# Rotary embedding over split heads: GpSimd's sine products taken two rows at a time

## The chip, the cores and the metric

The kernel runs on one core of a Trainium2 chip. The metric is the device time of the whole kernel in microseconds (us); lower is better. Three runs of the kernel before gave 161.14, 161.40 and 161.66 us, median 161.4 us.

## The reference

`x` is 16 batches x 512 positions x 1024 numbers (16 heads of 64), `cos` and `sin` are 512 x 32, everything fp32. Each head is split into halves x1 and x2 of 32 numbers, and

```
x    = x.reshape(16, 512, 16, 64);  x1, x2 = x[..., :32], x[..., 32:]
cos  = cos[None, :, None, :];       sin = sin[None, :, None, :]
out  = concatenate([x1*cos - x2*sin,  x1*sin + x2*cos], axis=-1)
```

So each number costs two products and a sum: its own value by the cosine, and its partner in the other half by plus or minus the sine. 33.6 MB are read and 33.6 MB are written.

## The kernel before, in words

**Rows.** The work is cut into 64 rows, numbered u = 0 to 63 (lists `rows`, `NU`). A row is 128 partitions x 1024 numbers: 4 KB in each partition. A tile is a load and a store: the first two and the last two batches are single tiles of 4 rows (2 MB), the twelve between go in six pairs of 8 rows (4 MB). Rows 0-3 and 4-7 are tiles 0 and 1, rows 8-15 to 48-55 are tiles 2 to 7, rows 56-59 and 60-63 are tiles 8 and 9. `x_sb` is a ring of 40 rows; results are written over the inputs and stored from there. Tiles 0 to 5 fill the ring and are loaded at once; tiles 6 to 9 wait for earlier stores.

**What a row goes through.**
- `mul` (VectorE, line 293): x times cosine into one of three PSUM buffers (`t1_ps`, NT1 = 3, slot u mod 3). It waits until row u-3 has left that buffer.
- The sine product: x with its halves swapped (a reversed axis, `::-1`) times the signed sine table, into one of six SBUF buffers (`t2_sb`, NT2 = 6, slot u mod 6). GpSimd does it at line 257 for 58 rows; VectorE does it at line 286 for the six rows that `V2` marks (r = 3 of each 8-row tile: 11, 19, 27, 35, 43, 51).
- The sum, in one of two ways. For 43 rows VectorE adds both products into `x_sb` (`comb`, line 304). For the 21 rows that `PE2` marks (4 <= u < 60 and u mod 8 in 1, 3, 6) TensorE adds the sine product into the PSUM buffer with a multiplication by the identity (line 224: two calls, four instructions), and ScalarE copies the buffer to `x_sb` (line 191).

**Order on the engines.** Each engine runs its list in order. VectorE's is written at line 311: for each u, `mul(u)` and then `comb(u-1)` unless row u-1 is TensorE's. Over eight rows of a tile, by r: mul0, comb7 of the tile before, mul1, comb0, mul2, (sine product 3) mul3, comb2, mul4, mul5, comb4, mul6, comb5, mul7. Because `t1_ps` has three slots, mul of r = 1 waits for ScalarE's copy of r = 6 of the tile before, mul4 for that of r = 1, mul6 for that of r = 3.

GpSimd goes through its 58 rows in order. Before each product it waits for the row's tile to be loaded (at r = 0, semaphore `sem_in`) and until row u-6 has released the slot of `t2_sb` (`wait_t2_free`, line 139): TensorE's semaphore `sem_e` if u-6 was a TensorE row, else VectorE's `sem_v` of that row's `comb`. After each product it counts up `sem_p`; `n_pool[u]` is the count that row u's reader waits for.

Loads are issued on ScalarE's queue (line 153), the later ones between its copies: after the copy of row 17, 25 and 33, with a wait for an earlier store (lines 192 to 195). Stores are issued on SyncE's queue (line 161) when a tile's last row and all before it are summed.

Of the kernel before, what the change touches and what calls it, by code (L numbers as in the profile page):

```python
# [6 lines left out]
def bass_split_heads_rope_kernel(  # L7
# [17 lines left out]
    H = int(num_heads)  # L25
    HD = dim // H
    HALF = HD // 2
    P = 128
    R1 = seq // P
# [5 lines left out]
    mult = mybir.AluOpType.mult  # L35
# [5 lines left out]
    tiles = [(b, R1 if b in singles else R2) for b in range(batch) if b in singles or b % 2 == 0]  # L41
# [4 lines left out]
    NU = len(rows)  # L46
# [5 lines left out]
    V2 = [tiles[t][1] == R2 and r == V_ROW for t, r in rows]  # L52

    def count(flags):
        return [sum(flags[: u + 1]) for u in range(NU)]

    n_pool = count([not v for v in V2])
    n_pe = count(PE2)
    n_comb = count([not a for a in PE2])

    NT1 = 3
    NT2 = 6
# [5 lines left out]
    with ExitStack() as stack:  # L68
        x_sb = stack.enter_context(nc.sbuf_tensor([P, RING, H, 2, HALF], fp32))
        t2_sb = stack.enter_context(nc.sbuf_tensor([P, NT2, H, 2, HALF], fp32))  # L70
        stage = stack.enter_context(nc.sbuf_tensor([P, 2, R1 * HALF], fp32))
        s1_sb = stack.enter_context(nc.sbuf_tensor([P, R1, 2, HALF], fp32))
        s2_sb = stack.enter_context(nc.sbuf_tensor([P, R2, 2, HALF], fp32))
# [17 lines left out]
        sem_m = stack.enter_context(nc.semaphore("mul"))  # L91
# [8 lines left out]

        def c_of(t, r):
            return c1_ps[:, r, :] if tiles[t][1] == R1 else pair_ps[:, r // R1, 0, r % R1, :]

        def s_of(t, r):
            return s1_sb[:, r] if tiles[t][1] == R1 else s2_sb[:, r]

        x1 = x.rearrange("b (s r) d -> b s (r d)", r=R1)
        o1 = out.rearrange("b (s r) h d -> b s (r h d)", r=R1)
# [13 lines left out]
        def where(u):  # L122
            t, r = rows[u]
            return t, r, u % RING

        def swapped(k):
            return x_sb[:, k, :, ::-1, :]

        def over_heads(table):
            return table[:, None, :, :].broadcast_to([P, H, 2, HALF])  # L130
# [8 lines left out]
        def wait_t2_free(eng, u):  # L139

            if u >= NT2:
                v = u - NT2
                if PE2[v]:
                    eng.wait_ge(sem_e, n_pe[v])
                else:
                    eng.wait_ge(sem_v, n_comb[v])
# [87 lines left out]
        def on_gpsimd(pl):  # L234
            pl.memset(ident[:], 1.0).then_inc(sem_i, 1)  # L235
            pl.wait_ge(sem_i, 1)
            pl.affine_select(  # L237
                out=ident[:],
                in_=ident[:],
                compare_op=mybir.AluOpType.is_equal,  # L240
                fill=0.0,
                base=0,
                pattern=[[-1, P]],
                channel_multiplier=1,
            ).then_inc(sem_i, 1)
            for u in range(NU):
                if V2[u]:
                    continue
                t, r, k = where(u)
                if (t, r) == (0, 0):  # L250
                    pl.wait_ge(sem_s, 1)
                if (t, r) == (2, 0):
                    pl.wait_ge(sem_s, 2)
                if r == 0:
                    pl.wait_ge(sem_in[t], 16)
                wait_t2_free(pl, u)
                pl.tensor_tensor(  # L257
                    t2_sb[:, u % NT2, :, :, :], swapped(k), over_heads(s_of(t, r)), mult
                ).then_inc(sem_p, 1)

        def on_vector(ve):
# [55 lines left out]
        on_sync(nc.sync)  # L317
        on_scalar(nc.scalar)
        on_gpsimd(nc.gpsimd)
        on_tensor(nc.tensor)  # L320
        on_vector(nc.vector)
# [33 lines left out]
```

## Time and profile before

| | |
|---|---|
| runs, us | 161.14, 161.40, 161.66 (median 161.4) |
| profiled execution: first to last instruction (span) | 160.3 us; its time with what lies around the span is not given apart, and the three runs lie 0.8 to 1.3 us above it |
| GpSimd, sine products, line 257 | x58, 2346 ns each, 134.2 us |
| VectorE, cosine products, line 293 | x64, 1.22 us each |
| VectorE, sums, line 304 | x43, 1.22 us each |
| VectorE, sine products, line 286 | x6, 1.21 us each |
| TensorE, sine into PSUM, line 224 | x84 instructions for 21 rows |
| ScalarE, copies, line 191 | x21, 1.02 us each |
| bytes moved | 67.26 MB, mean 419 GB/s over the span |
| loads / stores | 6 of 4 MB and 4 of 2 MB / the same |

The profile is of one execution. "Busy" counts the instructions of an engine; the number behind "idle before" is the time in which the engine stood still ahead of an instruction, and the name behind the arrow is what ended it. A timeline line reads: start, duration (of the whole merged group), engine, line, operation, written<-read, shapes, count.

### The profile page before, as it was taken

The numbers are of one execution on the slowest core, as the hardware profiler recorded it, in microseconds if no ns is written. First come the engines' busy times: TensorE is split into PE (matmuls) and PEld (weight loads), VectorE is DVE, ScalarE is ACT, GpSimd is POOL, SyncE is SP. The second block draws the span as 40 slices with busy tenths as digits, with TensorE's granted clock in tenths as the row PEclk, the third lists the DMA queues.
The fourth block names the chain that finished last, engine by engine and source line by source line (L and its number), as shares of the span: only waits on it lengthen the run. The fifth ranks groups of instructions, "written<-read, shape, count | busy, mean of one in ns | idle before, by whom it ended". The sixth has DMA issues, their size and how long they took to land.

```text
span 160.3 us, 522 instructions
## 1 busy us (share of the span) xinstructions
PE 72.8 (45%) x94; PEld 24.0 (15%) x94; DVE 130.3 (81%) x117; ACT 24.4 (15%) x27; POOL 134.9 (84%) x64
## 2 busy tenths in 40 slices
PE   6050004478357936660847105489458435850000
PEld 1020002022202211210221002022202111220000
DVE  0069998599989999996999709899889999999500
ACT  0420000203120222022012010201220402040000
POOL 1059999999999999999999999699999999289400
PEclk9955555557755587689687965555555977699555
DMA  5999999999999999999999999999999999999896
GB/s 147 409 441 474 409 450 409 425 429 429 446 429 458 417 411 466 409 433 401 450 433 425 425 409 458 409 433 433 411 429 462 441 417 401 450 441 441 376 450 294
DMA packets 3170, 67.26 MB, mean 419 GB/s; under 512 B 352, under 2 KB 608, under 8 KB 608
## 3 DMA queue, kind: packets, MB, share of 16 engines
q10 hardware_dynamic: 1728, 33.69, 49.6%
q1 hardware_dynamic: 1440, 33.56, 48.9%
q14 instruction: 2, 0.02, 0.0%
HBM read 33.69 MB, written 33.55 MB: 419 GB/s over the span
## 4 chain that ended last, share of the span: by engine, by line
DMA 60%; POOL 13%; DVE 8%; PE 7%; issue 3%; ACT 2%; ACTq 1%; DVEq 0%
DMA x_sb<-in_x_dram 41%; DMA out_dram<-x_sb 18%; POOL t_sb L257 13%; PE t_ps L224 7%; DVE t_ps L293 5%; DVE x_sb L304 3%; ACT x_sb L191 2%; ACTq L153 1%; ACTq L174 1%; DVE t_sb L286 0%; DVEq L303 0%
## 5 line engine op out<-in xcount | busy, mean ns | idle before, releaser
L257 POOL TENSOR_TENSOR t_sb<-x_sb,s_sb 128x1024 f32<-128x1024 f32 x58 | 134.2, 2346 | 14.8 <-ACT s_sb L183 8.5
L224 PE MATMUL t_ps<-t_sb,ident 128*128 128x512 f32 x84 | 68.0, 957 | 63.0 <-DVE t_ps L293 39.2
L293 DVE TENSOR_TENSOR t_ps<-x_sb,pair_ps 128x1024 f32<-128x1024 f32 x48 | 57.7, 1223 | 9.9 <-ACT x_sb L191 9.8
L304 DVE TENSOR_TENSOR x_sb<-t_ps,t_sb 128x1024 f32<-128x1024 f32 x43 | 52.4, 1218 | 2.6 <-POOL t_sb L257 2.6
L224 PEld LDWEIGHTS t_ps<-t_sb,ident 128*128 128x128 f32 x84 | 22.1, 290 | 108.9 <-DVE t_ps L293 74.6
L191 ACT ACTIVATE x_sb<-t_ps 128x1024 f32<-128x1024 f32 x21 | 21.5, 1023 | 109.9 <-PE t_ps L224 96.9
L293 DVE TENSOR_TENSOR t_ps<-x_sb,tab_ps 128x1024 f32<-128x1024 f32 x16 | 19.3, 1222 | 0.1
L286 DVE TENSOR_TENSOR t_sb<-x_sb,tab_ps 128x1024 f32<-128x1024 f32 x6 | 7.3, 1213 | 0.0
L264 DVE COPY tab_ps<-stage 128x128 f32<-128x128 f32 x1 | 0.3, 294 | 7.8 <-DMA stage<-in_cos_dram 7.8
L208 PE MATMUL pair_ps<-stage,pick 128*128 128x256 f32 x4 | 2.0, 667 | 5.4 <-DMA stage<-in_sin_dram 5.4
L201 PE MATMUL t_ps<-zero 128*128 128x512 bf16 x6 | 2.7, 627 | 1.3 <-DVE zero L262 1.3
L208 PEld LDWEIGHTS pair_ps<-stage,pick 128*128 128x128 f32 x4 | 1.2, 324 | 6.4 <-issue 6.3
L177 ACT ACT_TABLE_LOAD x1 | 1.3, 1283 | 5.5 <-issue 5.5
L201 PEld LDWEIGHTS t_ps<-zero 128*128 128x128 bf16 x6 | 0.7, 136 | 2.4 <-DVE zero L262 1.2
L262 DVE MEMSET zero<- 128x256 uint32 x1 | 0.3, 272 | 0.9 <-PEq L337 0.9
L186 ACT ACTIVATE s_sb<-pair_ps 128x256 f32<-128x256 f32 x1 | 0.4, 383 | 1.7 <-PE pair_ps L208 1.7
L182 ACT ACTIVATE s_sb<-stage 128x128 f32<-128x128 f32 x1 | 0.3, 309 | 2.1 <-DMA stage<-in_sin_dram 2.1
L235 POOL MEMSET ident<- 128x128 f32 x1 | 0.2, 204 | 0.3 <-POOLq L337 0.3
L177 ACT ACTIVATE pick<-ident 128x256 f32<-128x256 f32 x1 | 0.4, 416 | 0.0
L187 ACT ACTIVATE s_sb<-pair_ps 128x256 f32<-128x256 f32 x1 | 0.4, 379 | 0.0
L237 POOL TENSOR_SCALAR_AFFINE_SELECT ident<-ident 128x128 f32<-128x128 f32 x1 | 0.3, 292 | 0.1
L337 POOL MEMSET const-float32-0.0<- 128x1 f32 x1 | 0.1, 98 | 0.3 <-issue 0.3
(6 smaller groups left out, 1.0 us busy)
## 6 DMA issues: line engine op xcount, KB each, us to landing
x_sb<-in_x_dram ACTq DMA_DIRECT2D x6, 4096.0 KB, 38.0
out_dram<-x_sb SPq DMA_DIRECT2D x6, 4096.0 KB, 25.0
x_sb<-in_x_dram ACTq DMA_DIRECT2D x4, 2048.0 KB, 22.6
out_dram<-x_sb SPq DMA_DIRECT2D x4, 2048.0 KB, 15.2
stage<-in_cos_dram ACTq DMA_DIRECT2D x1, 64.0 KB, 7.8
stage<-in_sin_dram ACTq DMA_DIRECT2D x1, 64.0 KB, 7.5
```

What stands on the lines that cost most here:

```text
L153: eng.dma_start(in_sbuf(t), in_dram(x1, x2, t)).then_inc(sem_in[t], 16)
L174: ae.dma_start(stage[:, i, :], table.rearrange("(s r) d -> s (r d)", r=R1)).then_inc(sem, 16)
L177: ae.activation(pick[:], ident[:].rearrange("q (s k) -> q k s", k=2)[:, :, :, None].broadcast_to([P, 2, P // 2, 2]), COPY).then_inc(sem_g, 1)
L186: ae.activation(s2[:, :, :, 0, :], pair_ps[:, :, 1, :, :], COPY, scale=-1.0)
L191: ae.activation(xs[:, u % RING, :], t1_ps[:, u % NT1, :], COPY).then_inc(sem_a, 1)
L201: pe.matmul(t1_ps[:, k, b * BANK:(b + 1) * BANK], zero[:, 0:P], zero[:], start=True, stop=True).then_inc(sem_w, 1)
L208: pe.matmul(pair_ps[:, k].rearrange("p c r d -> p (c r d)"), pick[:, k].rearrange("q s b -> q (s b)"), stage[:].rearrange("q c f -> q (c f)"),
L224: ins = pe.matmul(t1_ps[:, u % NT1, b * BANK:(b + 1) * BANK], ident[:], t2[:, b * BANK:(b + 1) * BANK], start=False, stop=True, skip_group ...
L257: pl.tensor_tensor(t2_sb[:, u % NT2, :, :, :], swapped(k), over_heads(s_of(t, r)), mult).then_inc(sem_p, 1)
L286: ve.tensor_tensor(t2_sb[:, u % NT2, :, :, :], swapped(k), over_heads(v_ps), mult)
L293: ve.tensor_tensor(t1_ps[:, u % NT1, :].rearrange("p (h d) -> p h d", d=HALF), x_sb[:, k, :, :, :].rearrange("p h t d -> p (h t) d"), c_of ...
L304: ve.tensor_tensor(xs[:, k, :], t1_ps[:, u % NT1, :], t2_sb[:, u % NT2, :, :, :].rearrange("p h t d -> p (h t d)"), add,).then_inc(sem_v, 1)
```

## The change

For a row u that is even, from 4 to 60, and not followed by a row of VectorE's (`joined`), GpSimd writes the sine products of u and u+1 with one instruction of 128 x 2048 elements into two neighbouring slots of `t2_sb`. There are 23 such pairs; 12 rows stay single (0 to 3, r = 2 of each 8-row tile, 62, 63), so 58 instructions become 35. In an 8-row tile the pairs are r = 0+1, 4+5, 6+7.

The wait for the slots changes with it. A pair with u+1 >= 6 no longer waits for the exact release of its slots; it waits once, for `sem_m` >= u - 1, which is the end of `mul(u-2)` on VectorE. (That mul itself had to wait until row u-5 had left its PSUM buffer, and so until row u-5's reader was through with `t2_sb`.) Single rows wait as before. Readers of u and of u+1 both wait for the one count that the pair's instruction makes.

```diff
-    n_pool = count([not v for v in V2])
+    def joined(u):
+        return u % 2 == 0 and R1 <= u < NU - 2 and not V2[u + 1]
+
+    G2 = [joined(u) or (u % 2 == 1 and joined(u - 1)) for u in range(NU)]
+    n_pool = count([not v and not (g and u % 2 == 1) for u, (v, g) in enumerate(zip(V2, G2))])
...
-                if V2[u]:
+                if V2[u] or (G2[u] and u % 2 == 1):
                     continue
                 t, r, k = where(u)
+                n = 2 if G2[u] else 1
...
-                wait_t2_free(pl, u)
+                if n == 2 and u + 1 >= NT2:
+                    pl.wait_ge(sem_m, u + 2 - NT2 + NT1)
+                elif n == 1:
+                    wait_t2_free(pl, u)
+                table = (s1_sb if tiles[t][1] == R1 else s2_sb)[:, r:r + n]
                 pl.tensor_tensor(
-                    t2_sb[:, u % NT2, :, :, :], swapped(k), over_heads(s_of(t, r)), mult
+                    t2_sb[:, u % NT2:u % NT2 + n],
+                    x_sb[:, k:k + n, :, ::-1, :],
+                    table[:, :, None, :, :].broadcast_to([P, n, H, 2, HALF]),
+                    mult,
                 ).then_inc(sem_p, 1)
```

More of the change, by code (lines that the diff above doesn't have):

```diff
@@ L102, in c_of @@
             return c1_ps[:, r, :] if tiles[t][1] == R1 else pair_ps[:, r // R1, 0, r % R1, :]
-        def s_of(t, r):
-            return s1_sb[:, r] if tiles[t][1] == R1 else s2_sb[:, r]
         x1 = x.rearrange("b (s r) d -> b s (r d)", r=R1)
```

## The prediction

> **What bounds the kernel now.** I read the page's busy shares and slices, then VectorE's and GpSimd's timelines, then the waits of the store queue.
>
> ```profile
> PE 72.8 (45%) x94; PEld 24.0 (15%) x94; DVE 130.3 (81%) x117; ACT 24.4 (15%) x27; POOL 134.9 (84%) x64
> ...
> POOL 1059999999999999999999999699999999289400
> ...
> DMA  5999999999999999999999999999999999999896
> ```
>
> The DMA engines are full from the second slice to the third last, so bytes (67.26 MB) set the floor. GpSimd has no gap until 100 us, and then a few. To lose time, the change has to delay the last store until the store queue runs dry; to gain, it has little room: the DMA's last slices (8, 9, 6) leave about 1 us.
>
> How much cover has the last store? In the trace it is issued at 151.70. The store of rows 56-59, ahead of it in the queue, lands at 155.48, the last at 160.31; its first packet starts at 154.28. So it waited in line, and a delay of one to three us may cost nothing.
>
> Now the compute that leads to that issue. VectorE's timeline in a late tile (rows 43 to 49):
>
> ```profile
> 109.53 2.35 DVE L293 TENSOR_TENSOR t_ps<-x_sb,pair_ps 128x1024 f32<-128x1024 f32 x2
> 111.79 1.22 DVE L304 TENSOR_TENSOR x_sb<-t_ps,t_sb 128x1024 f32<-128x1024 f32 x1
> 113.42 1.23 DVE L293 TENSOR_TENSOR t_ps<-x_sb,pair_ps 128x1024 f32<-128x1024 f32 x1 [0.41 <-ACT x_sb L191]
> 114.56 1.22 DVE L304 TENSOR_TENSOR x_sb<-t_ps,t_sb 128x1024 f32<-128x1024 f32 x1
> 115.69 2.35 DVE L293 TENSOR_TENSOR t_ps<-x_sb,pair_ps 128x1024 f32<-128x1024 f32 x2
> 117.95 1.22 DVE L304 TENSOR_TENSOR x_sb<-t_ps,t_sb 128x1024 f32<-128x1024 f32 x1
> 119.58 1.23 DVE L293 TENSOR_TENSOR t_ps<-x_sb,pair_ps 128x1024 f32<-128x1024 f32 x1 [0.41 <-ACT x_sb L191]
> ```
>
> These are mul44+45, comb44, mul46, comb45, mul47+48, comb47, mul49. VectorE starts an operation every 1.13 us (113.42, 114.56, 115.69), so its 14 operations per 8-row tile take 15.9 us. Twice here it stands 0.41 us for ScalarE's copy: mul46 ends at 114.65, TensorE starts row 46 at 114.70, ScalarE copies it from 118.52 to 119.54, and mul49 starts at 119.58. That way (4.93 us from mul end to the next mul) is already 0.41 us longer than what VectorE has to do meanwhile. **Any delay of TensorE's row r = 6 goes straight into VectorE.** GpSimd's timeline at the same place:
>
> ```profile
> 101.72 9.29 POOL L257 TENSOR_TENSOR t_sb<-x_sb,s_sb 128x1024 f32<-128x1024 f32 x4 [1.78 <-PE t_ps L224]
> 111.39 6.97 POOL L257 TENSOR_TENSOR t_sb<-x_sb,s_sb 128x1024 f32<-128x1024 f32 x3 [0.38 <-DMA x_sb<-in_x_dram]
> 118.56 18.54 POOL L257 TENSOR_TENSOR t_sb<-x_sb,s_sb 128x1024 f32<-128x1024 f32 x8 [0.21 <-PE t_ps L224]
> 141.02 9.27 POOL L257 TENSOR_TENSOR t_sb<-x_sb,s_sb 128x1024 f32<-128x1024 f32 x4 [3.92 <-DMA x_sb<-in_x_dram]
> ```
>
> Rows 44 to 47 are done from 101.72 to 111.01, row 46 by 108.70: some 6 us before TensorE takes it up. At the end GpSimd has finished row 59 and waits 3.92 us for the last load.
>
> **Cost of a pair.** Four rows took 9.27 us: a start every 2.31 us, 2.346 us each. Two singles take 2.31 + 2.35 = 4.66 us at most. An instruction's fixed part is not shown by itself; GpSimd's affine_select of 128 x 128 takes 0.292 us with its elements, so at most 0.29 is saved: at least 4.37 (nothing in the row says that 2048 elements run faster than 2 x 1024). I take 4.55 to the end, 4.52 to the next start, nearer to the rows of the same operation. The instructions themselves so give back about 0.1 us per pair, 2.3 us over 23 pairs, of GpSimd's time, none of it on a path that sets the end unless GpSimd is the bound. The Trainium skill, "GPSIMD Engine Reference", section 3.1, gives 4497 ns for 2048 fp32 elements of such an operation; by it a pair is 4.50 and the loop below 0.05 shorter, an estimate that no run here shows yet.
>
> **The new wait.** Before, row 44 started when TensorE released row 38 (101.7). Now pair 44+45 waits for mul42, which in this trace ends at 106.23: 4.5 us later. Pair 46+47 waits for mul44 (110.75) and for the pair ahead of it. Behind each waiting pair stands all of GpSimd's list. Six slots no longer give six rows of lead; a pair is ready about 4.65 us after mul(u-2). Who feels it, by r:
> - comb0 and comb4 come 5 VectorE operations (5.65 us) after the end of mul6 and of mul2: hidden by 1 us.
> - TensorE's r = 1 waits for mul1, later than its pair: hidden.
> - **TensorE's r = 6** could start 3 operations (3.4 us) after mul4 ends, when mul6 is done. Its pair is ready only 4.65 us after it. And pair 4+5, started 0.1 after mul2, ends as mul4 does (sine 3, mul3, comb2, mul4: 4.53 us), so 6+7 gets no earlier start.
>
> So a loop closes: mul2 ends, 0.1, pair 4+5 (4.52), pair 6+7 (4.55), 0.14 to TensorE, 3.83 to ScalarE's copy (114.70 to 118.52), 1.02 + 0.04, then mul1, comb0, mul2 of the next tile (3.49). Sum **17.7 us per tile against 16.3** before (15.9 + 0.41): 1.4 lost per tile. A cheaper pair shortens only one of the two terms, since 6+7 waits for mul4 anyway.
>
> **Where that is absorbed, and where not.** Walking the loop from row 4: mul17 comes at 50.9 (before 47.5), mul25 at 68.4 (63.7), mul33 at 86.0 (81.0). There ScalarE's queue hides it:
>
> ```profile
> 93.08 2.40 ACTq L153 DMA_DIRECT2D x_sb<-in_x_dram  x2
> 95.52 1.02 ACT L191 ACTIVATE x_sb<-t_ps 128x1024 f32<-128x1024 f32 x1 [8.86 <-issue]
> ```
>
> The two last loads wait for a store that lands at 93.06, ScalarE copies row 35 only after them, and mul38 waited 5.31 us for it, until 96.58. By my walk VectorE reaches mul38 at 96.2: the 5 us lost are covered, with 0.4 to spare. Loads issued late elsewhere (row 17's copy at 56 instead of 53; the load queue is full until 72.3) cost nothing.
>
> After 96.58 nothing covers. Walked (before in brackets): pair 38+39 ends 98.65, mul41 103.7 (102.73); pair 46+47 ends 116.4 (row 46: 108.70), copy of 46 ends 121.4, mul49 121.4 (119.58); pair 54+55 ends 134.1, copy of 54 at 3.5 us (its own row) ends 138.8, mul57 138.8 (135.56). GpSimd then runs 56+57, 58+59, 60+61 without a pause: 138.65, 143.2, 147.7; the last load (140.96) is no longer what it waits for. Tail: comb60 at 147.8 (143.55), since row 60 waits for the pair with 61; then mul62, comb61, mul63, comb62, comb63, five starts of 1.13 and 1.22: 154.7. The last store is issued at **154.75 against 151.70, 3.05 us late**.
>
> From issue to end: by now the store of 56-59 lands near 155.5, so the last one stands almost alone.
>
> ```profile
> SPq L162 <- DMA out_dram<-x_sb: 8.3, 1, 8.3
> ```
>
> A 2 MB transfer took 8.0 us from issue to landing with nothing ahead of it (the first load, the least of all landings), and the last store 8.6 with 3.8 us of another before it. Ends: the first load's first packet came 1.0 us after its issue, the first store's 3.4 (between busy loads); the last store needed 6.0 from first packet to landing: 7.0 to 9.4. I take 8.0: 154.75 + 8.0 = 162.75 of span, and 1.1 around it (161.4 less 160.3): **163.8 us**. In the Trainium skill, "SBUF — State Buffer", section "The DMA setup-cost knee", a transfer is 2 us plus bytes at 436 GB/s: 6.8 us here, against the row's 8.0; the sum would be 162.6 by it. For the forecast alone, 7.0 and 9.4 give 162.8 and 165.2.
>
> **Rivals.**
> 1. *The store queue hides it: 161.4.* The last store's packets started at 154.28; with 1.0 us from issue to packet, an issue up to about 153.2 is free. What decides is TensorE's row 6: it took 3.83 us at a granted clock of 0.50, but rows at a clock of 0.91 took 2.0 (row 51: 125.39 to 127.41). If r = 6 gets that clock, the loop is 15.9 and only the tail remains: comb60 2.1 later by the pair, issue at 152.5 to 152.7. Against: rows 38, 41, 46 all took 3.8, and a later tile leaves TensorE idle longer. 0.15.
> 2. *The cover at row 35 is spent: 166.* If a pair takes 4.7 or the loop is 0.2 longer, mul38 comes 0.5 late, and three tiles and three pairs at the end add 1.2: issue at 156.5, and with 8.6 behind it 165.1 + 1.1. A pair dearer than two singles (nothing excludes that a four-dimensional operand costs more) gives more, to 168. 0.14.
> 3. *It doesn't do what it says: faster.* If GpSimd were the bound and a pair saved its full 0.29, tiles would take 15.9 and the end would meet the DMA's floor, 160.4 to 160.8. Against: DVE and TensorE's way to the copy, not GpSimd, set the late tiles. 0.06.
>
> **Numbers.** Forecast 0.65, own range 162.4 to 165.2. A difference under 0.3% (0.5 us) cannot be told from none here. Slower 0.79 (forecast and rival 2), same 0.15, faster 0.06. The range goes down to rival 1 and up to rival 2: 161.3 to 166.2; it leaves out rival 3 and the upper part of rival 2, and some of rival 1's lower side.
>
> **What would show it.** Right: GpSimd's waits name VectorE's line 293 (about 4 us each between singles and pairs 0+1 and 4+5 of late tiles); TensorE's waits for line 257 grow; VectorE's for line 191 grow to about 1.5 us per tile; mul41 to mul57 are 17.6 us per 8 rows; the wait of 5.31 at mul38 shrinks below 1; last store near 154.8. Wrong: mul49 within 0.5 us of 119.6; a pair outside 4.37 to 4.69; a last store before 153; mul38 later than 97.5.

## The result, and the profile after

The changed kernel takes 162.9 us in the median of four runs (162.29 to 163.38) against 161.47 before; the ratio is 1.0096, 95% interval 1.0069 to 1.0124: slower by 0.7 to 1.2%. The profiled execution took 162.93 us, with a span of 161.5. (In what follows medians are over all executions of a kernel, while ratios leave out executions over 1.5% above that kernel's fastest, so the two can differ where a kernel's times scatter.)

The head of the page of the changed kernel, and then its two forms of line 263 among the groups (busy us, mean ns of one, idle time before and what ended it):

```profile
PE 76.4 (47%) x94; PEld 24.5 (15%) x94; DVE 130.3 (81%) x117; ACT 24.4 (15%) x27; POOL 132.0 (82%) x41
...
DMA  5999999999999999999999999999999999999995
GB/s 142 402 454 463 406 430 434 479 394 390 446 475 442 390 448 454 398 446 406 422 414 454 430 390 430 471 398 410 450 450 390 430 422 450 479 398 414 430 398 227
```

```profile
L263 POOL TENSOR_TENSOR t_sb<-x_sb,s_sb 128x2048 f32<-128x2048 f32 x23 | 103.6, 4524 | 10.4 <-DVE t_ps L302 10.4
...
L263 POOL TENSOR_TENSOR t_sb<-x_sb,s_sb 128x1024 f32<-128x1024 f32 x12 | 28.1, 2354 | 8.3 <-ACT s_sb L184 8.3
```

A pair takes 4.52 us where two singles took 4.66 from the start of the first to the end of the second. GpSimd is busy for 2.9 us less (132.0 against 134.9), and stands 10.4 us for VectorE's cosine products, which it never waited for before. GpSimd's and VectorE's timelines in the tile that the prediction looked at:

```profile
98.56 6.84 POOL L263 TENSOR_TENSOR t_sb<-x_sb,s_sb 128x2048 f32<-128x2048 f32 x2 [1.10 <-DVE t_ps L302]
106.91 15.84 POOL L263 TENSOR_TENSOR t_sb<-x_sb,s_sb 128x2048 f32<-128x2048 f32 x4 [1.51 <-DVE t_ps L302]
124.27 27.10 POOL L263 TENSOR_TENSOR t_sb<-x_sb,s_sb 128x2048 f32<-128x2048 f32 x7 [1.52 <-DVE t_ps L302]
```

```profile
110.14 2.35 DVE L302 TENSOR_TENSOR t_ps<-x_sb,pair_ps 128x1024 f32<-128x1024 f32 x2
112.40 1.22 DVE L313 TENSOR_TENSOR x_sb<-t_ps,t_sb 128x1024 f32<-128x1024 f32 x1
113.82 1.23 DVE L302 TENSOR_TENSOR t_ps<-x_sb,pair_ps 128x1024 f32<-128x1024 f32 x1 [0.21 <-ACT x_sb L192]
114.96 1.22 DVE L313 TENSOR_TENSOR x_sb<-t_ps,t_sb 128x1024 f32<-128x1024 f32 x1
116.09 2.35 DVE L302 TENSOR_TENSOR t_ps<-x_sb,pair_ps 128x1024 f32<-128x1024 f32 x2
118.36 1.22 DVE L313 TENSOR_TENSOR x_sb<-t_ps,t_sb 128x1024 f32<-128x1024 f32 x1
120.70 1.23 DVE L302 TENSOR_TENSOR t_ps<-x_sb,pair_ps 128x1024 f32<-128x1024 f32 x1 [1.12 <-ACT x_sb L192]
```

GpSimd starts pair 44+45 at 106.91, right behind mul42, where before it started row 44 at 101.72. Its merged lines show the new rhythm: four instructions from 106.91, then 1.52 us of standing for VectorE. In VectorE's lines the stand ahead of mul49 has grown from 0.41 to 1.12 us: ScalarE's copy of row 46 comes at 119.64, since pair 46+47 ends at 115.95 and mul46 already at 115.05. mul41, mul49 and mul57 start at 103.34, 120.70 and 137.91: 17.36 and 17.21 us per tile, where before it was 16.85 and 15.98 (102.73, 119.58 and 135.56).

The last load no longer sets when GpSimd takes up row 60 (it lands at 140.87, and pair 60+61 starts at 142.23 behind the pairs ahead). The last store is issued at 153.81, where before it was 151.70.

So the loop is there. What made the end later is the harder question, and the experiments changed the answer.

### The profile page after: what moved, and what is told of

Read it like the earlier page. It is cut to its first block, busy times and chain, and to the rows that moved or that the text cites. A ratio compares the mean times of both kernels' runs of the same rounds, so it can differ in the third digit from the quotient of the medians.

```text
span 161.5 us, 499 instructions
## 1 busy us (share of the span) xinstructions
PE 76.4 (47%) x94; PEld 24.5 (15%) x94; DVE 130.3 (81%) x117; ACT 24.4 (15%) x27; POOL 132.0 (82%) x41
## 4 chain that ended last, share of the span: by engine, by line
POOL 41%; DMA 21%; PE 12%; DVE 10%; issue 6%; ACT 4%; ACTq 1%; DVEq 0%
POOL t_sb L263 41%; DMA out_dram<-x_sb 17%; PE t_ps L225 12%; DVE t_ps L302 5%; DVE x_sb L313 5%; DMA stage<-in_sin_dram 5%; ACT x_sb L192 4%; ACTq L154 1%; ACTq L175 0%; ACT s_sb L183 0%; ACT s_sb L184 0%; DVEq L312 0%; DVEq L147 0%
## 5 line engine op out<-in xcount | busy, mean ns | idle before, releaser
L263 POOL TENSOR_TENSOR t_sb<-x_sb,s_sb 128x2048 f32<-128x2048 f32 (+1 forms) x35 | 131.3, 3780 | 18.7 <-DVE t_ps L302 10.4
L225 PE MATMUL t_ps<-t_sb,ident 128*128 128x512 f32 x84 | 71.6, 1003 | 62.0 <-POOL t_sb L263 35.0
L225 PEld LDWEIGHTS t_ps<-t_sb,ident 128*128 128x128 f32 x84 | 22.6, 297 | 110.9 <-DVE t_ps L302 59.1
L192 ACT ACTIVATE x_sb<-t_ps 128x1024 f32<-128x1024 f32 x21 | 21.5, 1024 | 112.4 <-PE t_ps L225 107.3
```

The source lines that it names most:

```text
L192: ae.activation(xs[:, u % RING, :], t1_ps[:, u % NT1, :], COPY).then_inc(sem_a, 1)
L225: ins = pe.matmul(t1_ps[:, u % NT1, b * BANK:(b + 1) * BANK], ident[:], t2[:, b * BANK:(b + 1) * BANK], start=False, stop=True, skip_group ...
L263: pl.tensor_tensor(t2_sb[:, u % NT2:u % NT2 + n], x_sb[:, k:k + n, :, ::-1, :], table[:, :, None, :, :].broadcast_to([P, n, H, 2, HALF]), ...
```

## The theories

**A**: a pair that starts only after mul(u-2) is ready too late for TensorE's row r = 6; it takes the late start and the double length together. **B**: the double length alone. **C**: the coarse wait alone. These differ in where the compute is delayed. From the compute to the end there are two ways: **A1**, the last store comes after the store queue has run dry; **A2**, later stores all along leave single ones of the 16 DMA engines behind, whatever the last store does. A1 is the prediction's; A2 arose from the first four runs.

| kernel | median, us | ratio to before, 95% interval |
|---|---|---|
| changed kernel | 162.9 | 1.0096 (1.0069 to 1.0124) |
| pairs, exact wait | 162.12 | 1.0039 (1.0009 to 1.0070) |
| singles, coarse wait | 161.29 | 0.9999 (0.9986 to 1.0012) |
| without pairs 6+7 | 161.39 | 1.0003 (0.9991 to 1.0016) |
| only pairs 6+7 | 163.01 | 1.0097 (1.0066 to 1.0127) |
| only pair 60+61 | 161.31 | 0.9994 (0.9974 to 1.0015) |
| before, last sum held back | 161.87 | 1.0033 (1.0010 to 1.0057) |
| changed kernel without pair 60+61 | 162.52 | 1.0068 (1.0038 to 1.0098) |
| exact wait without pair 60+61 | 161.79 | 1.0001 (0.9979 to 1.0024) |
| before, six stores held back | 163.56 | 1.0069 (1.0034 to 1.0103) |
| before, only the first three held back | 166.15 | 1.0121 (1.0082 to 1.0160) |
| before, only the last three held back | 161.29 | 0.9995 (0.9966 to 1.0023) |
| changed kernel, wait one mul longer | 176.41 | 1.0929 (1.0903 to 1.0955) |

The kernel before took 161.47 us in the median of the first comparison and 161.22 to 161.37 in the others.

## Experiments on the compute: which part of the change delays

**Pairs with the exact wait.**

```diff
-                if n == 2 and u + 1 >= NT2:
-                    pl.wait_ge(sem_m, u + 2 - NT2 + NT1)
-                elif n == 1:
-                    wait_t2_free(pl, u)
+                wait_t2_free(pl, u)
+                if n == 2:
+                    wait_t2_free(pl, u + 1)
```

> The pairs stay; before a pair GpSimd waits for the exact release of both slots (readers of rows u-6 and u-5) instead of for mul(u-2). Theory A (a pair that starts only after mul(u-2) is ready too late for TensorE's row 6 of each tile; it needs the late start and the double length together): pair 46+47 starts at about 108 when row 41 is through TensorE, ends near 112.5, ahead of mul46; mul41 to mul49 to mul57 go back to 16.3 us per tile; only the pair 60+61 still costs about 0.9 us of the last store's issue, which the store queue covers: 161.3 to 161.8. Theory B (double length alone, or the 2048-element instruction disturbing the other engines): stays at 162.9. Theory C (the coarse wait alone): 161.4.

Measured: 162.12, spread from 161.2 to 163.6 without the two slowest (163.75 and 167.36). GpSimd's timeline of the late tiles:

```profile
102.07 4.51 POOL L262 TENSOR_TENSOR t_sb<-x_sb,s_sb 128x2048 f32<-128x2048 f32 x1 [3.22 <-DVE x_sb L312]
107.28 20.28 POOL L262 TENSOR_TENSOR t_sb<-x_sb,s_sb 128x2048 f32<-128x2048 f32 x5 [0.70 <-PE t_ps L225]
```

Pair 44+45 starts at 102.07 and 46+47 at 107.28, 4.8 and 4.2 us earlier than with the coarse wait, and mul41, mul49, mul57 come at 102.34, 118.44, 134.45: 16.1 and 16.0 us per tile. As A said, the late loop is gone. The time is not back to 161.4, though, and where the rest comes from is not shown. The early tiles are late: mul17 is at 48.89 against 47.51 before. But the profiled execution, in which that is so, took 161.20 us, no longer than before.

**Singles with the coarse wait.**

```diff
-                wait_t2_free(pl, u)
+                if joined(u) and u + 1 >= NT2:
+                    pl.wait_ge(sem_m, u + 2 - NT2 + NT1)
+                elif not (u % 2 == 1 and joined(u - 1)):
+                    wait_t2_free(pl, u)
```

> 58 single products as before, but with the changed kernel's wait: the even row of a would-be pair waits for mul(u-2), the odd one for nothing more. Theory A: row 46 is ready 2.35 us, not 4.5, after its start; by the sum about 7.0 us after mul42's end against mul46's end at 7.9, so TensorE is not held up: 16.3 us per tile, 161.4. Theory B: 161.4. Theory C (the coarse wait alone costs the time): 162.9.

Measured: 161.29, no difference. C falls: the coarse wait by itself is free. One of its thirteen executions took 165.45 us; the profile is of that one, and even there the late tiles take 16.35 and 16.83 us.

**Without the pairs 6+7, and with nothing else.** The two edits of `joined`:

```diff
-        return u % 2 == 0 and R1 <= u < NU - 2 and not V2[u + 1]
+        return u % 2 == 0 and R1 <= u < NU - 2 and not V2[u + 1] and u % R2 != 6
```

```diff
-        return u % 2 == 0 and R1 <= u < NU - 2 and not V2[u + 1]
+        return u % R2 == 6 and R1 <= u < NU - 2
```

> The changed kernel without the pairs 6+7 of each tile (those rows are single, with the exact wait). Theory A: the loop over TensorE's row 6 is open, 16.3 us per tile, the last store some 1 us late by pair 60+61 and covered: 161.3 to 161.8. Theory B: 15 of 23 pairs are left, so about two thirds of the 1.4 us: 162.3. Theory C: about 162.3 too.

> Only the pairs 6+7 of each tile (7 pairs), all other rows single with the exact wait. Theory A: pair 6+7 waits for mul4 and ends 4.6 us after it, where mul6 ends 3.4 after: the loop is as long as with all pairs, 17.2 to 17.5 us per tile; the tail has no pair, but GpSimd comes late to it: last store 153.2, 162.2 to 162.8. Theory B and C: 7 of 23 pairs, so about a third of 1.4 us: 161.8.

Measured: 161.39 without them (16 of the 23 pairs are left, no loss), and 163.01 with these seven alone (the whole loss). One of the twelve executions without them took 214.45 us, for a reason that is not known. B falls as the cause of the whole loss (the double length costs at most what the exact wait left, 0.1 to 0.7%), and the place is settled: the pair that holds TensorE's row r = 6. With the seven alone, mul41, mul49 and mul57 are at 102.70, 120.31 and 137.39, 17.6 and 17.1 us apart. But this run broke something else in my reasoning. Its last store goes out at 152.81, a full microsecond before the changed kernel's, and yet its profiled span is 162.3 against 161.5. The GB/s line of the page before, and the DMA lines of this run's page:

```profile
GB/s 147 409 441 474 409 450 409 425 429 429 446 429 458 417 411 466 409 433 401 450 433 425 425 409 458 409 433 433 411 429 462 441 417 401 450 441 441 376 450 294
```

```profile
DMA  5999999999999999999999999999999999999992
GB/s 145 412 448 448 436 416 404 485 392 420 432 485 408 404 487 404 420 469 396 428 469 396 404 444 428 428 452 396 473 396 404 436 491 396 404 485 388 412 444 97
```

There is no gap ahead of the last store: 388, 412, 444 GB/s in the slices before the last. Then the last slice (4.06 us) moves only 97 GB/s, where before it moved 294: a few engines are still at work when the rest are done. A DMA counts its semaphore up 16 times, presumably once per engine, and the trace has the time of each count. Of the last store 14 counts are in by 160.01 (before: by 160.16), the last two at 161.29 and 162.23. That is no store queue run dry.

**Double the wait.** `pl.wait_ge(sem_m, u + 3 - NT2 + NT1)`, so that a pair waits for mul(u-1).

> The changed kernel with every pair waiting one mul longer, for mul(u-1): double the suspected wait. Theory A: the loop over TensorE's row 6 grows by one VectorE step, 1.13 us, from 17.3 to 18.4 us per tile; row 38 then is no longer covered by the wait for the loads (about 99.9 instead of 97.2), and mul57 comes near 143; last store about 159, 166 to 168.5. If the wait were not on the path: 162.9 as the changed kernel.

Measured: 176.41, far over what I expected, because I had put the new step into the wrong arm of the loop. VectorE's timeline of one tile:

```profile
111.79 1.23 DVE L302 TENSOR_TENSOR t_ps<-x_sb,pair_ps 128x1024 f32<-128x1024 f32 x1 [2.48 <-ACT x_sb L192]
...
122.24 1.23 DVE L313 TENSOR_TENSOR x_sb<-t_ps,t_sb 128x1024 f32<-128x1024 f32 x1 [1.30 <-POOL t_sb L263]
...
131.60 1.23 DVE L302 TENSOR_TENSOR t_ps<-x_sb,pair_ps 128x1024 f32<-128x1024 f32 x1 [2.48 <-ACT x_sb L192]
```

From mul41 (111.79) to mul49 (131.60) it is 19.8 us, 2.45 more than in the changed kernel. Pair 4+5 now waits for mul3 instead of mul2, and between them VectorE also does its own sine product: two operations of 1.13 us, 2.27 together, on the longer arm. The wait is on the path, and its price per tile follows from counting VectorE's operations between the two muls.

## Experiments on the end: from late sums to a late kernel

**Only the pair 60+61**: `joined` returns `u == NU - 4`.

> Only the pair 60+61 is left; every other product is single with the exact wait. By the sum in the prediction the last store goes out at about 152.6 instead of 151.7, within the store queue's cover (the store before it lands at 155.5, and a store needs about 1 us to its first packet). Theory A1 (the loss is made at the very end: the last store comes after the store queue has run dry) and theory A2 (later stores all along the late tiles leave single DMA engines behind, whatever the last store does): both 161.2 to 161.7. If the end alone, through the pair 60+61, made the loss: 162.9.

Measured: 161.31. The last store goes out at 151.98; the tail pair is covered.

**The kernel before, last sum held back.** Ahead of comb63:

```diff
+                if u == NU:
+                    ve.wait_ge(sem_v, n_comb[NU - 3])
+                    for j in range(3):
+                        ve.wait_ge(sem_m, NU + j)
+                        ve.tensor_tensor(
+                            t1_ps[:, (NU - 3) % NT1, :].rearrange("p (h d) -> p h d", d=HALF),
...
+                        ).then_inc(sem_m, 1)
+                    ve.wait_ge(sem_m, NU + 3)
```

> The kernel before, with three idle products of VectorE put in front of the very last sum (extra work, written to a PSUM buffer that nobody reads any more). Only the last store is later: issued at about 153.9 instead of 151.7, as in the changed kernel (153.8), while all earlier stores keep their times. Theory A1: 162.3 to 162.9. Theory A2: below 161.9.

Measured: 161.87, 0.5 us over before. Its last store is issued at 154.54, 0.7 us later even than the changed kernel's, and the store queue does run dry:

```profile
DMA  5999999999999999999999999999999999999977
GB/s 147 414 437 468 424 432 399 456 428 407 444 415 493 405 407 472 391 424 448 407 448 440 407 456 432 399 415 436 434 436 448 428 411 428 468 424 428 403 334 326
```

334 and 326 in the last two slices are a gap that all engines share (at 155.0 one packet is under way where 16 are usual), and then a full end. A1 is real, but a store that is 2.8 us late costs 0.5, not 1.4. Standing alone, the last 2 MB need only 6.3 us from issue to the span's end (160.9 less 154.54).

**The changed kernel without pair 60+61** (`R1 <= u < NU - 4`), and **the exact wait without it**.

> The changed kernel with rows 60 and 61 single; the loop in the tiles ahead stays. GpSimd comes out of rows 58+59 at about 142.3 and ends row 63 at 151.6: last store at 153.0 instead of 153.8. Theory A1: 0.4 to 0.8 us less than the changed kernel, 162.1 to 162.5. Theory A2: 162.9.

> Pairs with the exact wait, rows 60 and 61 single: neither the loop nor the late tail. Last store at 151.7. Theories A1 and A2: 161.2 to 161.6, so the 0.8 us that the exact wait left over would have come from the pair 60+61. If it stays near 162.1, the pairs cost something else, in the tiles ahead.

Measured: 162.52 (+1.2 over before), with the last store out at 152.60, which the run above and the one with pair 60+61 alone say is nearly free; its last slice moves 93 GB/s, again the picture of engines left behind. So most of the loss is there with a last store whose delay is nearly free: A1 alone falls. The exact wait without the pair is inconclusive: 161.79, but a ratio of 1.0001 with an interval that reaches from -0.2 to +0.2%, and its times scatter from 161.1 to 167.1.

**The kernel before, with stores held back.** The engines' work is untouched; SyncE waits for one row more before it issues the store of an 8-row tile:

```diff
-                    wait_added(sp, u)
+                    wait_added(sp, u + 1 if 2 <= t <= 7 else u)
```

and `2 <= t <= 4` and `5 <= t <= 7` in the two runs that split it.

> The kernel before, its engines untouched, but SyncE holds the store of each 8-row tile until the row after it is summed too: each of these six stores is issued about 2.4 us later (49.9, 66.0, 83.4, 105.1, 121.9, 137.9 instead of 47.5, 63.7, 81.1, 102.7, 119.6, 135.6), about as in the kernels with the loop; the last two stores keep their times. Theory A2 (later stores along the tiles leave single DMA engines behind): 161.9 to 162.6, one to three engines ending past 160.5 while the rest end at 159.2. Theory A1 (only the last store counts): 161.2 to 161.6.

> As the run with all six 8-row stores held back for one row, but only for the first three (rows 8 to 31, issued at 49.9, 66.0, 83.4). If the stragglers among the DMA engines are made while stores fall behind the loads between 50 and 95 us, this has most of the loss: 161.8 to 162.4. If the stores after 100 us make them: 161.2 to 161.5.

> Only the last three 8-row stores held back (rows 32 to 55, issued at 105.1, 121.9, 137.9). If the stragglers come from the stores after 100 us: 161.8 to 162.4. If from those before: 161.2 to 161.5.

Measured: all six held back 163.56 (161.3 to 169.4); the first three alone 166.15 (163.4 to 169.2); the last three alone 161.29. Holding back three stores of rows 8 to 31 by 1.9 to 2.9 us, with no engine's work changed, makes the kernel slower by 4.8 us in the median, more than the whole change did, and it does so in all seven executions: the fastest took 163.44. With all six held back, though, the same three among them, three of twelve executions took no longer than before (161.32 to 161.52); why the other three seem to help is not shown. GpSimd's timeline with the first three held back, and the page's DMA slices:

```profile
113.07 16.23 POOL L257 TENSOR_TENSOR t_sb<-x_sb,s_sb 128x1024 f32<-128x1024 f32 x7 [2.11 <-DMA x_sb<-in_x_dram]
129.65 9.29 POOL L257 TENSOR_TENSOR t_sb<-x_sb,s_sb 128x1024 f32<-128x1024 f32 x4 [0.36 <-DMA x_sb<-in_x_dram]
145.04 9.27 POOL L257 TENSOR_TENSOR t_sb<-x_sb,s_sb 128x1024 f32<-128x1024 f32 x4 [6.10 <-DMA x_sb<-in_x_dram]
```

```profile
DMA  5999999999999999999999999999999999999592
GB/s 147 409 444 442 494 387 431 403 419 446 466 391 502 393 407 470 399 446 438 399 478 399 431 415 423 438 403 431 456 423 391 431 458 415 454 407 431 223 407 120
```

The DMA is full until 152 us, as before. But a load's wait is over only when its semaphore has counted to 16 (line 153), and the loads land later and later although the mean of the engines is full: GpSimd takes up row 48 at 113.07 (before 111.39), and the last tile at 145.04 (before 141.02). There is a simpler rival: the loads of rows 48 to 63 wait for the first two of the held-back stores, so they may just have been issued late. They were, by 0.1 and 0.5 us (73.72 and 93.60 against 73.60 and 93.08), but 14 of the last load's 16 counts were in by 139.70, earlier than before (140.76), and the last only at 144.98 (before 140.96). So what is late is an engine or two and not the load as a whole. Then the other engines run out of stores (223 GB/s in the third last slice) while that tile is computed, and what is late at the end is both.

The same counts tell whether this is what the changed kernel has too. The table gives how many us the 16th count of a store came after its 8th, and the span of the profiled execution that these counts are from:

| kernel | rows 16-23 | rows 32-39 | rows 48-55 | last store | span, us |
|---|---|---|---|---|---|
| only pair 60+61 | 2.06 | 0.64 | 0.25 | 0.22 | 159.7 |
| pairs, exact wait | 1.08 | 0.62 | 0.31 | 0.28 | 159.8 |
| before, only the last three held back | 0.69 | 0.25 | 0.36 | 0.32 | 159.9 |
| exact wait without pair 60+61 | 0.81 | 0.14 | 0.70 | 0.69 | 160.1 |
| before | 1.02 | 0.57 | 0.36 | 0.33 | 160.3 |
| before, last sum held back | 1.33 | 0.71 | 0.88 | 0.11 | 160.9 |
| before, six stores held back | 1.85 | 1.32 | 1.50 | 1.50 | 161.1 |
| changed kernel | 2.42 | 1.78 | 1.71 | 1.43 | 161.5 |
| only pairs 6+7 | 1.61 | 2.55 | 2.69 | 2.70 | 162.3 |
| changed kernel without pair 60+61 | 1.76 | 2.91 | 2.92 | 2.92 | 162.5 |
| before, only the first three held back | 1.07 | 3.63 | 4.43 | 2.41 | 164.4 |

In the first six the engines come together again; in the last five some are 1.5 to 4.4 us behind at rows 48 to 55 and stay behind to the end. In the changed kernel half of the last store's counts are in by 160.05, as before (159.98); the last comes at 161.48 instead of 160.31. So A2's picture is shown, in the changed kernel as well: single engines left behind, long before the last store goes out. In the kernel before, holding back the stores of rows 8 to 31 brings it about, and holding back the last three alone does not. But late stores are not the only way to it: the execution of 165.45 us above has it too (4.10 at rows 48 to 55), with these stores on time (47.49, 63.52, 81.67).

## Why the prediction came out as it did

- **The pair's price**: 4.55 to its end, 4.52 to the next start; measured 4.52, and 4.47 to 4.49 where the next pair waits for nothing (115.91 to 120.39). Right.
- **The loop over TensorE's row 6**: shown by taking the pairs 6+7 away (no loss), leaving them alone (all of it), taking the coarse wait or the double length away (the late loop opens). Sized at 17.7 us per tile, measured 17.61 in the early tiles (mul9 at 32.86, mul17 at 50.47, mul25 at 68.08) and 17.36 and 17.21 in the late ones; there a tile lost 0.5 and 1.2 us, not 1.4. The term that was too large is TensorE's: 0.14 + 3.83 us from the pair's end to the copy, measured 3.69 (115.95 to 119.64), at a granted clock of 0.70 from 104 to 121 us where it was 0.50 before. By mul57 the sum was 138.8; measured 137.91.
- **The cover at row 35**: half right. mul38 was to come at 96.6, in the shadow of the two loads. It came at 97.18 after a wait of 2.06 us, not below 1, because the store that these loads wait for landed at 95.17 instead of 93.06: the shadow itself moved with the late stores, and mostly with that store's last two counts (14 of the 16 were in by 93.47).
- **The last store**: 154.75 predicted, 153.81 measured, the loop's smaller term carried on.
- **From issue to end**: 8.0 us, measured 7.67 in the changed kernel, but 6.3 for a last store that really stands alone, below the lower bound of 7.0: that bound borrowed 6.0 us from a store that had still been queueing behind another. By it the changed kernel's last store would have ended the span at 160.1, no later than before. The charge of 2.4 us (163.8 against 161.4) for the last store's delay is the step that failed: held back further still, it cost 0.5. That half of the last store's counts came at 160.05 says the same.
- **"Loads issued late elsewhere ... cost nothing"**, and the view behind it that everything up to 96.58 is covered: this failed too. The delay of the stores of rows 8 to 31 (issued at 50.5, 68.1, 84.8 instead of 47.5, 63.7, 81.1) was taken as free, since the DMA stays full. The runs with held-back stores show that such a delay alone can cost as much as the whole change and more. That the sum came near the result is luck: an overcharged end stood in for an uncharged middle. The compute part, up to the issue of the last store, was right in its main mechanism and 0.94 us too long.
- **A sign that missed**: GpSimd was to stand about 4 us at a time for VectorE. It stood 0.9 to 1.8 us: its list, with the pairs ahead, runs late itself.

Two things stay open. That in the changed kernel it is the late stores of rows 8 to 31 which leave engines behind is inferred: no other stores did so when held back alone, and its engines are apart from these stores on (2.41 us at rows 8 to 15, 1.13 before); a kernel with the loop in the late tiles alone was not run. And why a single engine falls behind when these stores come later, and why some 2.4 us there did more harm than the 3 to 4.4 us of the changed kernel, none of the runs tells. No version here beats the kernel before.

## What to carry to other kernels

Before joining two instructions of a producer, ask for each consumer how long after the new, shared wait it wants its half; here one consumer in eight rows had 3.4 us where a pair needs 4.65, and those seven pairs made all of the loss. A coarse wait alone was free here, and long instructions with the exact wait cost 0.1 to 0.7%: together they made a loop over four engines and cost 0.7 to 1.2%. And in a kernel whose DMA is full from end to end, don't book a delayed store as free: hold the stores back by themselves and measure, since the end is set by the slowest of the DMA engines and not by their mean.

## What the runs showed of the hardware that was not expected

- The 16 DMA engines drift apart, and loads land and the kernel ends with the last of them: with the same bytes, the last slice moved 294 GB/s before, 97 with the seven pairs and 120 with three stores held back, and the last store's 16 counts came 0.33, 2.70 and 2.41 us apart from the 8th on. Holding back three 4 MB stores by some 2.4 us cost from 2.1 to 7.8 us, depending on the execution (163.44 to 169.17 against a median of 161.37).
- On GpSimd a product of 2048 elements in a partition takes 4524 ns where one of 1024 takes 2354. If time grows evenly with the elements, about 0.18 us of an instruction is fixed (an estimate: twice 2354 less 4524).
- A 2 MB store takes 6.3 us from issue to landing when nothing is ahead of it: 168.63 to 174.96 with the wait one mul longer, where the DMA stood empty, and 154.54 to 160.88 with the last sum held back.
